# Gate matrices of the expert layer from bfloat16 one-hots, eight tokens at a time, made on VectorE

## The chip, the core and the metric

The kernel runs on one NeuronCore of one Trainium2 chip. The time is device microseconds of one execution from start to end; the median of the runs counts. A core has five engines with queues of their own: TensorE (PE; its weight loads are listed apart as PEld), VectorE (DVE), ScalarE (ACT), GpSimd (POOL) and SyncE (SP), which here only issues DMAs.

## What is computed

Two transformer blocks over 512 tokens of width 1024, in float32. The change lies in the expert layer of the first block. There each token gets, from each of 8 heads, 16 experts out of 128 x 128, each with a softmax weight; expert number 128 i + j is found from two lists of 128 sub-keys.

```
fv, fi = lax.top_k(cand, PEER_TOPK)
idx = jnp.take_along_axis(cidx, fi, axis=-1)
g = jax.nn.softmax(fv, axis=-1)
a = jax.nn.gelu(jnp.einsum('chkd,cd->chk', u_tab[idx], xc), approximate=False)
out = jnp.einsum('chkd,chk->cd', v_tab[idx], g * a)
```

A token thus has 128 triples (i, j, g). Instead of gathering rows, the kernel gives each token a dense 128 x 128 gate matrix, with g at the places (i, j) that were chosen (summed, if one is chosen twice) and zero elsewhere.

## The kernel before, in words

The first block's mixers come first, then the expert layer, then the second block. Float32 products that need full accuracy are split: `wload` (L125) loads a weight (SP), rounds it to `whi` on ScalarE (L130) and takes the rest `wlo` on VectorE (L132), and `mm3` (L135) makes three matmuls (L136 to L138) of the parts.

In the expert layer token tile 0 (128 tokens) gathers the rows of its experts: `gather_steps` (L458) has 256 steps, each an indirect DMA from POOL (L464, L473) and a sum over 1024 elements on VectorE (L466, L475). The other three tiles meet all experts densely. `h_block` (L445) computes the activations of 128 experts for 384 tokens: one `wload`, 24 matmuls of 384 columns, and one Gelu on ScalarE (L450). 68 such blocks are made during the routing and are parked in HBM (L455, `park_blocks`).

`decode` (L540) turns a tile's top-16 lists into three 128 x 128 arrays with a token's selections along the row: i, j and the weight g. It transposes them on TensorE (L584), and ScalarE copies the result out as `sT` (L586) and, negated, as `nT` (L588). After that a partition is a selection and a column is a token.

`gate_matrix` (L591) makes the gates of 16 tokens; it is called 8 times for each of tiles 1 to 3, 24 times in all. It works in chunks of 8 tokens. VectorE compares the row `io` of 0 to 127 with the 8 tokens' j: `oj`, 8 x 128 float32 (L596). For each token `og` is made, the one-hot of i times g: on VectorE in one operation (L606) or on ScalarE in two (L609, L610); `ON_DVE` (L30) says which of four tokens go to VectorE: two in tile 1, three in tiles 2 and 3. One matmul with `oj` as weights and `og` as the moving operand (L612) gives the token's 128 x 128 matrix. Four of them fill a PSUM bank, ScalarE copies the bank into `stg`, where the tokens are innermost (L614), and after 16 tokens SP stores 1 MB into `wdr` in HBM (L615).

What orders the work: the calls stand in program order, and a scheduler at build time orders each engine's instructions, with what comes first in the program preferred. After each `gate_matrix` come one or two parked blocks (`PARKS`, L26) and up to three gather steps (`GATH`, L27), and the decodes of tiles 0, 2 and 3 stand between groups (`DECODE`, L29). After the last group the parked blocks that are left follow, then the dense phase from L705, whose order is written out by hand: it reads `wdr` back, 8 rows of experts at a time, multiplies the activations by it and makes the product with the second expert table. It needs PSUM banks that the gate matrices use until their end.

Of the kernel before, what the change touches and what calls it, by code (L numbers as in the profile page):

```python
# [22 lines left out]
NEG = -1e30  # L23
NPARK = 68                                # blocks of expert activations computed during the routing
NLEAD = 3                                 # blocks in front of the parked ones
PARKS = ((), (2, 1), (2, 2), (2, 1))      # parked blocks per group of a tile's gate matrix, even and odd  # L26
GATH = (0, 1, 3, 3)                       # gathers per group of a tile's gate matrix  # L27
RATE = (0.9, 2.5)                         # gathers per dense block, parked and not
DECODE = {(1, 1): 0, (1, 4): 2, (2, 3): 3}  # L29
ON_DVE = ((), (0, 2), (0, 1, 2), (0, 1, 2))  # L30
INV_FREQ = [1.0, 0.1939227432012558, 0.03760603070259094, 0.007292664609849453,
# [10 lines left out]
def body(ctx: ExitStack, tc: tile.TileContext, A: dict, out: bass.AP):  # L42
# [13 lines left out]
    def sqrt_ahead(after):  # L56
        """Has the activation table of Sqrt loaded before the chain that needs it."""
        w = sm.tile([128, 1], F32, name="warm", bufs=1)
        SC.activation(w, after, AF.Square)
        SC.activation(w, w, AF.Sqrt)  # L60
# [13 lines left out]
    def rstd_newton(var, which):  # L74
        """1 / sqrt(var + eps) by three Newton steps from the exponent-halving guess, on the vector engine alone."""
        w = sm.tile([128, 4], F32, name="nw")
        x, y, a, r = [w[:, k:k + 1] for k in range(4)]
        V.tensor_scalar(x, var, (1e-5, 1e-6)[which], None, op0=OP.add)
        V.tensor_scalar(a.bitcast(U32), x.bitcast(U32), 1, None, op0=OP.logical_shift_right)
        V.tensor_scalar(y.bitcast(U32), a.bitcast(U32), -1.0, 1597463007.0, op0=OP.mult, op1=OP.add)  # L80
        for c in (-3.0, -12.0, -768.0):
            V.scalar_tensor_tensor(a, x, y, y, op0=OP.mult, op1=OP.mult)
            V.scalar_tensor_tensor(y, a, c, y, op0=OP.add, op1=OP.mult)
        V.tensor_scalar(r, y, -1.0 / 8192.0, None, op0=OP.mult)
        return r
# [14 lines left out]
    def first_half(junk_pool, y):  # L100
        """mean square of a row's first half, halved, plus the norm's eps"""
        ss = sumsq(junk_pool, y, 512)
        b = sm.tile([128, 1], F32, name="half")
        V.tensor_scalar(b, ss, 1.0 / D, 1e-6, op0=OP.mult, op1=OP.add)
        return b
# [49 lines left out]
    def halves(mm_pool, srcs, xh, xl, fill, parts=(0, 1)):  # L155
        """The blocks of srcs, two token tiles ahead of the other two; fill() readies those."""
        ws = [wload(src, [128, ND, 128]) for src in srcs]
        pss = [mm_pool.tile([128, S], F32, name="mm", tag="mm") for _ in srcs]
        for part in parts:
            sl = slice(part * 256, part * 256 + 256)  # L160
            if part == parts[1]:
                fill()
            for (wh, wl), ps in zip(ws, pss):
                fm_block(ps[:, sl], wh, wl, xh[:, :, sl], xl[:, :, sl], ND)
        return pss
# [25 lines left out]

    # ------------------------------------------------ first block: mixers
    with ExitStack() as st:
# [201 lines left out]

    # ------------------------------------------------ product-key experts
    # token tile 0 gathers its expert rows; the other tiles meet every expert on the tensor engine
    with ExitStack() as st:
# [87 lines left out]
        with mix as s1:  # L486
# [18 lines left out]
            for hp_ in range(16):  # L505
# [19 lines left out]
                if hp_ % 2 == 0:  # L525
                    continue
                # a pair (a, b) has (a + 1)(b + 1) - 1 pairs before it in the order, so b < 4 once a >= 4
                h = hp_ // 2
# [11 lines left out]
            def decode(t):  # L540
# [42 lines left out]
                for k, y in enumerate((sel[0], sel[1], gw)):  # L583
                    PE.transpose(tp[:, k, :], y, ident)  # L584
                sT = rt.tile([128, 3, 128], F32, name="sT", bufs=2)
                SC.activation(sT, tp[:, 0:3, :], AF.Copy)  # L586
                nT = rt.tile([128, 3, 128], F32, name="nT", bufs=2)
                SC.activation(nT, tp[:, 0:3, :], AF.Copy, scale=-1.0)  # L588
                return sT, nT

            def gate_matrix(t, q, sT, nT):  # L591
                stg = rw.tile([128, 128, TG], F32, name="stg", bufs=2)
                for c in range(TG // 8):
                    t8 = q * TG + 8 * c
                    oj = rw.tile([128, 8, 128], F32, name="oj", bufs=2)
                    V.tensor_tensor(oj, io[:, None, :].to_broadcast([128, 8, 128]),  # L596
                                    sT[:, 1, t8:t8 + 8, None].to_broadcast([128, 8, 128]), op=OP.is_equal)
                    for e in range(2):
                        pool, tag = ((psw, "wps"), (pmm, "mm"))[e]
                        ps = pool.tile([128, 4, 128], F32, name="wps", tag=tag)  # L600
                        for k in range(4):
                            tok = t8 + 4 * e + k
                            dve = k in ON_DVE[t]
                            og = rw.tile([128, 128], F32, name="og", tag="ogv" if dve else "oga", bufs=6)
                            if dve:
                                V.tensor_scalar(og, io, sT[:, 0, tok:tok + 1], sT[:, 2, tok:tok + 1],  # L606
                                                op0=OP.is_equal, op1=OP.mult)
                            else:
                                SC.activation(og, io, AF.Abs, bias=nT[:, 0, tok:tok + 1])  # L609
                                SC.activation(og, og, AF.Relu, scale=nT[:, 2, tok:tok + 1],  # L610
                                              bias=sT[:, 2, tok:tok + 1])
                            PE.matmul(ps[:, k, :], lhsT=oj[:, 4 * e + k, :], rhs=og)  # L612
                        o = 8 * c + 4 * e
                        SC.activation(stg[:, :, o:o + 4].rearrange("p i t -> p t i"), ps, AF.Copy)  # L614
# [5 lines left out]
            quick.close()  # L620
            rw = s1.enter_context(tc.tile_pool(name="rw", bufs=2, reuse_waits="tile"))
            ahead = {1: decode(1)}
            for t in range(1, NT):
                for q in range(128 // TG):
                    if (t, q) in DECODE:
                        n = DECODE[t, q]
                        ahead[n] = decode(n)
                    gate_matrix(t, q, *ahead[t])
            spread(parks, NPARK)

# [116 lines left out]

    # ------------------------------------------------ second block
    with ExitStack() as st:
# [347 lines left out]
```

## Time and profile before

| | |
|---|---|
| median of 3 runs | 2314.72 us (2312.84 to 2319.04) |
| span of the profiled execution | 2313.5 us (its page has no other time) |
| TensorE, matmuls | 2246.8 us busy, 97% of the span |
| VectorE | 1495.2 us, 65% |
| ScalarE | 986.1 us, 43% |
| GpSimd | 382.4 us, 17% |
| gate matrices (first to last matmul of L612) | 589.9 to 874.9 us |

The span runs from the first to the last instruction. A busy time is the time in which an engine had an instruction in work; matmuls overlap, so the duration of one is longer than the step from one start to the next, and in a run the step is what counts. "Idle before" names the time an engine stood still ahead of a group and what it waited for. The clock is TensorE's granted clock as a share of full speed.

### The profile page before, as it was taken

What the parts mean: (1) busy time and instruction counts of PE and PEld (TensorE: products, weight loads), DVE (VectorE), ACT (ScalarE), POOL (GpSimd) and SP (SyncE); (2) the same over time, 40 slices, a digit from 0 to 9 for tenths busy, and PEclk for the clock granted to TensorE, in tenths of its full rate; (3) what the DMA queues carried; (4) which work ended last, traced back from release to release, by engine and by line L of the source; (5) the groups of instructions that cost most, each with busy time, mean ns of one, the idle gap of its engine ahead of it and who ended that gap; (6) DMA issues with size and microseconds to landing.
All of it is one profiled execution on the core that took longest, in us unless ns stands there. A gap on an engine that the chain in (4) does not pass through costs nothing.

```text
span 2313.5 us, 30184 instructions
## 1 busy us (share of the span) xinstructions
PE 2246.8 (97%) x11337; PEld 1931.4 (83%) x11337; DVE 1495.2 (65%) x2998; ACT 986.1 (43%) x1631; POOL 382.4 (17%) x261
## 2 busy tenths in 40 slices
PE   7999998999899999999999999999999999999998
PEld 6768887989799999777779999999976778888886
DVE  4553254989999994767777777777784555333323
ACT  4354233333897783333333333333353364322222
POOL 0000000000222430323323444444400000000000
PEclk9999999999899999999999999999999999999999
DMA  5202232443577997889899898889732112333331
GB/s 173 92 19 75 90 111 84 128 125 118 213 272 289 363 350 253 295 311 329 293 323 322 306 320 297 296 302 323 274 113 74 56 55 87 105 101 93 98 100 65
DMA packets 177572, 444.82 MB, mean 192 GB/s; under 512 B 15249, under 2 KB 84241, under 8 KB 174353
## 3 DMA queue, kind: packets, MB, share of 16 engines
q1 hardware_dynamic: 140560, 308.65, 39.8%
q0 software_dynamic: 36864, 134.23, 16.3%
q8 instruction: 89, 1.46, 0.2%
q14 instruction: 59, 0.48, 0.1%
HBM read 402.19 MB, written 40.63 MB: 191 GB/s over the span
## 4 chain that ended last, share of the span: by engine, by line
PE 86%; DVE 5%; ACT 4%; DMA 4%; issue 1%; DVEq 0%; ACTq 0%; SPq 0%
PE mm L136 13%; PE mm L137 12%; PE mm L138 12%; PE hps L138 7%; PE hps L136 7%; PE hps L137 7%; PE acc L136 6%; PE acc L138 6%; PE acc L137 6%; DMA wraw<-in_v_experts_dram 3%; PE wps L612 2%; PE sc L311 1%; PE pv L346 1%; ACT stg L614 1%; PE sc L889 1%
## 5 line engine op out<-in xcount | busy, mean ns | idle before, releaser
L130 ACT ACTIVATE whi<-wraw 128x1024 fp32r<-128x1024 f32 x232 | 241.8, 1045 | 568.9 <-PE mm L137 343.0
L132 DVE TENSOR_TENSOR wlo<-wraw,whi 128x1024 fp32r<-128x1024 f32 x232 | 278.7, 1204 | 265.9 <-ACT whi L130 261.5
L136 PE MATMUL hps<-x2h,whi 128*128 128x384 f32 x1024 | 348.1, 340 | 2.1 <-ACT whi L130 1.8
L138 PE MATMUL hps<-x2h,wlo 128*128 128x384 f32 x1024 | 345.1, 337 | 0.8 <-DVE wlo L132 0.8
L137 PE MATMUL hps<-x2l,whi 128*128 128x384 f32 x1024 | 344.2, 336 | 0.0
L464 POOL DMA_INDIRECT gu<-in_u_experts_dram,ix x128 | 190.8, 1491 | 914.0 <-PE wps L612 605.5
L136 PE MATMUL acc<-whi,hh 128*128 128x512 f32 x768 | 302.6, 394 | 17.3 <-ACT hh L117 17.3
L138 PE MATMUL acc<-whi,hl 128*128 128x512 f32 x768 | 303.2, 395 | 0.0
L137 PE MATMUL acc<-wlo,hh 128*128 128x512 f32 x768 | 302.7, 394 | 0.0
L664 DVE TENSOR_TENSOR wlo<-wraw,whi 128x1024 fp32r<-128x1024 f32 x188 | 227.5, 1223 | 74.6 <-ACT whi L662 69.0
L662 ACT ACTIVATE whi<-wraw 128x1024 fp32r<-128x1024 f32 x188 | 198.3, 1056 | 171.3 <-issue 85.5
L473 POOL DMA_INDIRECT gv<-in_v_experts_dram,ix x128 | 189.7, 1482 | 380.7 <-DVE hres L475 275.3
L136 PEld LDWEIGHTS hps<-x2h,whi 128*128 128x128 f32 x1024 | 193.3, 189 | 5.4 <-ACT whi L130 2.1
L137 PEld LDWEIGHTS hps<-x2l,whi 128*128 128x128 f32 x1024 | 193.1, 189 | 2.7
L138 PEld LDWEIGHTS hps<-x2h,wlo 128*128 128x128 f32 x1024 | 193.1, 189 | 1.1 <-DVE wlo L132 1.1
L136 PEld LDWEIGHTS acc<-whi,hh 128*128 128x128 f32 x768 | 145.5, 189 | 49.6 <-ACT hh L117 21.0
L138 PEld LDWEIGHTS acc<-whi,hl 128*128 128x128 f32 x768 | 145.8, 190 | 33.3 <-DVE hl L118 2.7
L137 PEld LDWEIGHTS acc<-wlo,hh 128*128 128x128 f32 x768 | 145.7, 190 | 29.3
L475 DVE SCALAR_TENSOR_TENSOR hres<-gv,ga,hres 128x1024 f32<-128x1024 f32 x128 | 164.1, 1282 | 1.0
L466 DVE CUSTOM_DVE_ANT_0 gu<-gu,xtok 128x1024 f32<-128x1024 f32 x128 | 154.5, 1222 | 0.0
L137 PE MATMUL mm<-x4l,whi 128*128 128x512 f32 (+1 forms) x384 | 143.9, 375 | 0.0
L136 PE MATMUL mm<-x4h,whi 128*128 128x512 f32 (+1 forms) x384 | 143.3, 376 | 0.3 <-ACT x4h L117 0.3
(316 smaller groups left out, 4022.3 us busy)
## 6 DMA issues: line engine op xcount, KB each, us to landing
wraw<-in_u_cols_dram SPq DMA_DIRECT2D x128, 512.0 KB
wraw<-in_v_experts_dram SPq DMA_DIRECT2D x128, 512.0 KB
wraw<-in_w_in_dram SPq DMA_DIRECT2D x50, 512.0 KB
wdr<-stg SPq DMA_DIRECT2D x24, 1024.0 KB
wt<-wdr SPq DMA_DIRECT2D x16, 1536.0 KB
park<-hg SPq DMA_DIRECT2D x68, 192.0 KB
hg<-park SPq DMA_DIRECT2D x68, 192.0 KB
wraw<-in_w_gate_dram SPq DMA_DIRECT2D x22, 512.0 KB
```

Of the source, the lines that this page charges most:

```text
L130: SC.activation(hi, raw, AF.Copy)
L132: V.tensor_tensor(lo, raw, f(hi), op=OP.subtract)
L136: PE.matmul(ps, lhsT=ah, rhs=bh, start=start, stop=False)
L137: PE.matmul(ps, lhsT=ah, rhs=bl, start=False, stop=False)
L138: PE.matmul(ps, lhsT=al, rhs=bh, start=False, stop=stop)
L464: GP.indirect_dma_start(out=u, out_offset=None, in_=A["u_experts"], in_offset=bass.IndirectOffsetOnAxis(ap=ix[:, s_:s_ + 1], axis=0))
L466: V.tensor_tensor_reduce(out=u, in0=u, in1=xtok, scale=1.0, scalar=0.0, op0=OP.mult, op1=OP.add, accum_out=a[:, s_:s_ + 1])
L473: GP.indirect_dma_start(out=v, out_offset=None, in_=A["v_experts"], in_offset=bass.IndirectOffsetOnAxis(ap=ix[:, s_:s_ + 1], axis=0))
L475: V.scalar_tensor_tensor(hres[:, 0, :], v, a[:, s_:s_ + 1], hres[:, 0, :], op0=OP.mult, op1=OP.add)
L612: PE.matmul(ps[:, k, :], lhsT=oj[:, 4 * e + k, :], rhs=og)
L662: SC.activation(hi, raw, AF.Copy)
L664: V.tensor_tensor(lo, raw, f(hi), op=OP.subtract)
```

## The change

`decode` copies i, j and g as bfloat16 (`sT`, five rows of 128): i and j are whole numbers below 128, g is kept as the sum of three bfloat16, each the rest that the one before it leaves. ScalarE makes the first copy, VectorE the two rests in four operations. `nT` is gone. `gate_matrix` makes, for a chunk of 8 tokens, the one-hots of i and of j in one VectorE operation (`hot`) and the three products of the first with the parts of g in another (`og`), in a layout with the 8 tokens innermost. Each token then takes three bfloat16 matmuls that add up in PSUM, whose operands step over the 8 tokens. `io8`, the numbers 0 to 127 each eight times, is made once. The ScalarE path and `ON_DVE` are gone. Apart from this only comments change.

```diff
@@ -582,34 +581,34 @@
                 tp = psw.tile([128, 4, 128], F32, name="wps", tag="wps")
                 for k, y in enumerate((sel[0], sel[1], gw)):
                     PE.transpose(tp[:, k, :], y, ident)
-                sT = rt.tile([128, 3, 128], F32, name="sT", bufs=2)
-                SC.activation(sT, tp[:, 0:3, :], AF.Copy)
-                nT = rt.tile([128, 3, 128], F32, name="nT", bufs=2)
-                SC.activation(nT, tp[:, 0:3, :], AF.Copy, scale=-1.0)
-                return sT, nT
-
-            def gate_matrix(t, q, sT, nT):
+
+                sT = rt.tile([128, 5, 128], BF16, name="sT", bufs=2)
+                SC.activation(sT[:, 0:3, :], tp[:, 0:3, :], AF.Copy)
+                rest = rt.tile([128, 128], F32, name="grest")
+                V.tensor_tensor(rest, tp[:, 2, :], sT[:, 2, :], op=OP.subtract)
+                V.tensor_copy(sT[:, 3, :], rest)
+                V.tensor_tensor(rest, rest, sT[:, 3, :], op=OP.subtract)
+                V.tensor_copy(sT[:, 4, :], rest)
+                return sT
+
+            def gate_matrix(t, q, sT):
                 stg = rw.tile([128, 128, TG], F32, name="stg", bufs=2)
                 for c in range(TG // 8):
                     t8 = q * TG + 8 * c
-                    oj = rw.tile([128, 8, 128], F32, name="oj", bufs=2)
-                    V.tensor_tensor(oj, io[:, None, :].to_broadcast([128, 8, 128]),
-                                    sT[:, 1, t8:t8 + 8, None].to_broadcast([128, 8, 128]), op=OP.is_equal)
+                    ts = slice(t8, t8 + 8)
+                    hot = rw.tile([128, 2, 128, 8], BF16, name="hot")
+                    V.tensor_tensor(hot, io8[:, None, :, :].to_broadcast([128, 2, 128, 8]),
+                                    sT[:, 0:2, None, ts].to_broadcast([128, 2, 128, 8]), op=OP.is_equal)
+                    og = rw.tile([128, 3, 128, 8], BF16, name="og")
+                    V.tensor_tensor(og, hot[:, 0, None, :, :].to_broadcast([128, 3, 128, 8]),
+                                    sT[:, 2:5, None, ts].to_broadcast([128, 3, 128, 8]), op=OP.mult)
                     for e in range(2):
                         pool, tag = ((psw, "wps"), (pmm, "mm"))[e]
                         ps = pool.tile([128, 4, 128], F32, name="wps", tag=tag)
                         for k in range(4):
-                            tok = t8 + 4 * e + k
-                            dve = k in ON_DVE[t]
-                            og = rw.tile([128, 128], F32, name="og", tag="ogv" if dve else "oga", bufs=6)
-                            if dve:
-                                V.tensor_scalar(og, io, sT[:, 0, tok:tok + 1], sT[:, 2, tok:tok + 1],
-                                                op0=OP.is_equal, op1=OP.mult)
-                            else:
-                                SC.activation(og, io, AF.Abs, bias=nT[:, 0, tok:tok + 1])
-                                SC.activation(og, og, AF.Relu, scale=nT[:, 2, tok:tok + 1],
-                                              bias=sT[:, 2, tok:tok + 1])
-                            PE.matmul(ps[:, k, :], lhsT=oj[:, 4 * e + k, :], rhs=og)
+                            for p in range(3):
+                                PE.matmul(ps[:, k, :], lhsT=hot[:, 1, :, 4 * e + k], rhs=og[:, p, :, 4 * e + k],
+                                          start=(p == 0), stop=(p == 2))
                         o = 8 * c + 4 * e
                         SC.activation(stg[:, :, o:o + 4].rearrange("p i t -> p t i"), ps, AF.Copy)
                 SY.dma_start(wdr[(t - 1) * (128 // TG) + q], stg)
@@ -619,13 +618,15 @@
 
             quick.close()
             rw = s1.enter_context(tc.tile_pool(name="rw", bufs=2, reuse_waits="tile"))
+            io8 = rw.tile([128, 128, 8], BF16, name="io8", bufs=1)
+            V.tensor_copy(io8, io[:, :, None].to_broadcast([128, 128, 8]))
             ahead = {1: decode(1)}
             for t in range(1, NT):
                 for q in range(128 // TG):
                     if (t, q) in DECODE:
                         n = DECODE[t, q]
                         ahead[n] = decode(n)
-                    gate_matrix(t, q, *ahead[t])
+                    gate_matrix(t, q, ahead[t])
             spread(parks, NPARK)
 
         dn = st.enter_context(tc.tile_pool(name="dn", bufs=2, reuse_waits="tile"))
```

## Rows read from the trace of the kernel before

**Rows 1.** The page, part 1: busy time, share of the span and instructions of each engine.

```profile
span 2313.5 us, 30184 instructions
...
PE 2246.8 (97%) x11337; PEld 1931.4 (83%) x11337; DVE 1495.2 (65%) x2998; ACT 986.1 (43%) x1631; POOL 382.4 (17%) x261
```

**Rows 2.** Windows of the gate stage: length, busy (instructions) per engine, clock, DMA share, GB/s.

```profile
587.00:691.00 104.00, 94.05 (x581) 90.08 (x582) 95.90 (x178) 97.92 (x200) 26.08 (x17) 0.94 0.71 253
691.00:794.00 103.00, 102.15 (x673) 100.91 (x672) 101.61 (x185) 79.07 (x144) 31.96 (x23) 1.00 0.88 323
794.00:877.00 83.00, 82.84 (x563) 82.15 (x562) 77.59 (x150) 64.80 (x114) 26.78 (x19) 1.00 0.94 348
877.00:900.00 23.00, 23.00 (x135) 23.00 (x134) 7.36 (x6) 8.25 (x11) 0.00 (x0) 1.00 0.83 272
```

**Rows 3.** Groups by shape, window 586:877: count, busy us, mean ns, idle before and its releasers.

```profile
L614 ACT ACTIVATE stg<-wps 128x512 f32<-128x512 f32 x96 | 101.9, 1079 | 2.5 <-PE wps L612 2.5
L612 PE MATMUL wps<-og,oj 128*128 128x128 f32 x768 | 99.5, 284 | 9.0 <-ACT og L610 6.9 <-DVE og L606 2.0
L612 PEld LDWEIGHTS wps<-og,oj 128*128 128x128 f32 x768 | 94.4, 196 | 14.5 <-ACT og L610 9.8 <-DVE og L606 2.1 <-PE hps L137 1.1
L606 DVE TENSOR_SCALAR og<-io,sT 128x128 f32<-128x128 f32 x256 | 72.0, 354 | 5.2 <-PE wps L612 3.9 <-PE hps L138 1.3
...
L596 DVE TENSOR_TENSOR oj<-io,sT 128x1024 f32<-128x1024 f32 x48 | 58.6, 1221 | 2.9 <-PE wps L612 2.8
L610 ACT ACTIVATE og<-og,sT,nT 128x128 f32<-128x128 f32 x128 | 58.2, 488 | 0.5
...
L609 ACT ACTIVATE og<-io,nT 128x128 f32<-128x128 f32 x128 | 46.2, 395 | 0.0
```

**Rows 4.** Time line of SyncE's queue in tile 3: start, duration, issue.

```profile
805.51 0.32 SPq L615 DMA_DIRECT2D wdr<-stg  x1
...
817.61 0.32 SPq L615 DMA_DIRECT2D wdr<-stg  x1
...
825.66 0.32 SPq L615 DMA_DIRECT2D wdr<-stg  x1
```

**Rows 5.** Time line of TensorE, tile 2: a block's matmuls, then the gate products.

```profile
749.72 0.33 PE L136 MATMUL hps<-x2h,whi 128*128 128x384 f32 x1
...
751.28 3.73 PE L612 MATMUL wps<-og,oj 128*128 128x128 f32 x32
754.77 0.42 PE L136 MATMUL hps<-x2h,whi 128*128 128x384 f32 x1
```

**Rows 6.** Time lines of TensorE: products of 512 columns; further on, products of 64.

```profile
1019.70 0.39 PE L138 MATMUL acc<-whi,hl 128*128 128x512 f32 x1
...
1023.78 0.39 PE L138 MATMUL acc<-whi,hl 128*128 128x512 f32 x1
...
1791.78 2.00 PE L915 MATMUL pv<-va,pt 128*128 128x64 f32 x16
```

**Rows 7.** Groups by shape, whole span: ScalarE's dense copy of 512 elements.

```profile
L520 ACT ACTIVATE rsc<-sc 128x512 f32<-128x512 f32 x16 | 9.6, 597 | 17.5 <-PE sc L518 17.5
```

**Rows 8.** Time line of VectorE in tile 2: one chunk and the next one's start.

```profile
752.21 1.63 DVE L606 TENSOR_SCALAR og<-io,sT 128x128 f32<-128x128 f32 x6
753.75 1.22 DVE L596 TENSOR_TENSOR oj<-io,sT 128x1024 f32<-128x1024 f32 x1
754.88 1.63 DVE L606 TENSOR_SCALAR og<-io,sT 128x128 f32<-128x128 f32 x6
```

**Rows 9.** Groups by shape, window 586:877: VectorE's bfloat16 operations in the decode.

```profile
L560 DVE TENSOR_TENSOR eq<-abf,io 128x2048 bf16<-128x2048 f32 x6 | 13.6, 2284 | 0.0
L563 DVE TENSOR_TENSOR eq<-eq,sif 128x2048 bf16<-128x2048 bf16 x6 | 7.2, 1218 | 0.0
L565 DVE TENSOR_TENSOR eq<-eq 128x1024 bf16<-128x1024 bf16 x6 | 4.0, 686 | 0.0
```

**Rows 10.** The same view: a small operation of the decode on 128 columns.

```profile
L576 DVE TENSOR_TENSOR gw<-gw,gs 128x128 f32<-128x128 f32 x3 | 0.9, 289 | 0.0
```

More of the change, by code (lines that the diff above doesn't have):

```diff
@@ L29 @@
 DECODE = {(1, 1): 0, (1, 4): 2, (2, 3): 3}
-ON_DVE = ((), (0, 2), (0, 1, 2), (0, 1, 2))
 INV_FREQ = [1.0, 0.1939227432012558, 0.03760603070259094, 0.007292664609849453,
```

## The prediction

> **What bounds the kernel now.** I read the page's first part, then the stretches of the stage that the change touches, then the groups of instructions in that stage, then time lines of TensorE and VectorE inside it. The page says that TensorE has work in 97% of the span [rows 1], so time comes mostly from TensorE's list of work, and an edit elsewhere counts only where TensorE waits. The gate matrices are made from about 587 to 877 us, in 24 groups of 16 tokens, eight groups for each of three token tiles. By tile the stage takes 104, 103 and 83 us [rows 2]. What to see there: in the first tile ScalarE is busy 97.92 of 104 us, TensorE 94.05, and its mean granted clock is 0.94. In the other two tiles TensorE is busy 102.15 of 103 and 82.84 of 83, ScalarE has a quarter free. VectorE is busy 95.90, 101.61 and 77.59, so it is nearly full everywhere: 275.1 of 290. So the first tile waits for ScalarE's half of the one-hots (the weight loads of L612 stood idle 14.5 us, most of it behind the og of L610 [rows 3]); the other two are TensorE's, with VectorE a hair behind. The start times of the gate stores in tile 3 show it: a group with two parked blocks takes 12.1 us, one with a single block 8.1 [rows 4]. The difference, 4.0, is one block of 24 matmuls at 0.173 us [rows 5]; the rest is the group's own matmuls.
>
> **Part 1, the matmuls.** The 384 products show as 768 float32 instructions of 128 columns [rows 3], two to a product. A run of 32 takes 3.49 us until the next block starts, 0.109 each; with its last result taken off, (3.73 - 0.28) / 31 = 0.111 [rows 5]. So 768 x 0.111 = 85 us of TensorE. The new code issues 3 x 384 = 1152 instructions, each with a weight load of its own, as today even two successive products of one weight have. What one bfloat16 instruction costs no row shows, so bounds. Below: split float32 products of 384 columns start every 0.173 us (1.56 over nine) and of 512 every 0.227 (4.08 over eighteen) [rows 5, 6]; so 128 columns in one pass are 0.054, and 0.173 - 3 x 0.054 = 0.011 stays per instruction: 0.065, which makes 75 us, 10 less than now. The float32 row is 0.111, two passes, and it does not fall with fewer columns: sixteen of 64 columns take 2.00 us, 0.115 each [rows 6], so there the weights set the pace.
>
> What speaks for the upper half is the layout. Both operands now step over eight tokens, 16 bytes from one element to the next, where today's are dense. The one strided writer in the stage pays for it: ScalarE's copy of 512 elements into the gate tile, in steps of 64 bytes, takes 1079 ns [rows 3], a dense copy of the same size from the same memory 597 [rows 7], 1.8 times as much. TensorE reading at twice the time per element would be at the pace of the float32 row, 0.111 to 0.12. Upper bound: the float32 row times 1.8, 0.20, or 231 us. I take 0.112, because the strided row is the only one that shows what such steps cost and a read of two passes is a row of this engine: 1152 x 0.112 = 129 us, **44 more than now**. [...]
>
> **Part 2, VectorE.** Removed in each chunk of eight tokens: one oj, started 1.13 us before what follows, and six og in 1.54 us in tiles 2 and 3 (752.21, 753.75, 754.88) [rows 8], together 2.67; in tile 1 only four og, about 2.16. Added: hot, 2048 bfloat16 elements, and og, 3072. The nearest rows are the decode's bfloat16 products: 2048 elements 1218 ns, 1024 elements 686, one of the two sources repeated in the first; with a float32 source 2284 [rows 9]. By their slope og is 1218 + 532 = 1750. Less 0.08 for the overlap that oj shows (1221 ns long [rows 3], next start after 1.13), a chunk is 1.14 + 1.67 = 2.81. That is 0.65 more in 16 chunks and 0.14 more in 32: 15 us. The decode's four new small operations on 128 columns, at about 0.29 each [rows 10], are 1.2 us in each of three tiles, and io8 about one oj, 1.1 us, once. Sum: **19 us more**, 294 us for a stage of 290. The other end, with no gain from bfloat16, is 2284 + 3426 ns per chunk: 131 us more than the 2.81.
>
> **Part 3, ScalarE.** Gone are 46.2 + 58.2 us of og [rows 3] and the negated copy. Of its 242 us some 137 stay. This pays only where TensorE waited for it: 290 - 279.0 = 11 us idle in the stage, and about 6 us of lost speed in tile 1 (granted 0.94 of 104 us) [rows 2]. What is late next is VectorE's og: it needs hot, and the four or eight products of a chunk need it, and behind a waiting product on TensorE stand parked blocks. hot and og have two buffers each, so VectorE's third hot waits for TensorE, and behind it stand the next wlo and the gathers' sums, whose buffers GpSimd waits for. Two chunks are one group, about 12 us ahead, which covers the two blocks of 4.1 us between groups. No DMA is added on SP's or POOL's queue, and stores and loads keep their order.
>
> **Sum.** TensorE's stage at full clock is 279.0 - 6.2 = 273 us; with 44 it is 317. At the start the new decode and io8 lie on the way to the first product, about 2 us, and I leave 1 us of other waits. 320 us against 290 is +30, and VectorE's 294 fits under it with room. Behind 877 the order is fixed and TensorE bounds, so all of it reaches the end: 2313.5 + 30 = 2344 of the profiled span. The page gives a span and no other time for that execution; the median of the runs, 2314.72, lies 1.2 above. **2345 us.**
>
> **Rivals.**
> - *VectorE becomes the bound.* If strided reads cost nothing, TensorE's stage is 273 - 10 = 263 and VectorE's 294 plus some 3 of waits lasts longer: 297 against 290, +7, about 2322, between +3 and +14. For it: VectorE is at 95% today and its new sum is sure in kind. It holds up to a matmul of about 0.09 us. Half of this case is within the 0.3%, 7 us, that a measurement here can tell from no change. Chance 0.28.
> - *Faster, the gathers step aside.* With 0.065 per product TensorE has 263 us of work, and no wait for ScalarE. It gains if VectorE sheds at least 26 of its 294 us: gathers that lag into 877 to 900, where VectorE is busy 7.36 of 23 [rows 2]. Then 263 + 2 + 3 = 268, -22, about 2293. Against it: the gathers stand ahead of the next group in program order, only 16 us are free there, and products must cost the lower bound. Chance 0.11.
> - *Far slower.* The bfloat16 operations don't run at the rate of the rows, so the change doesn't do what it says: 294 + 131 = 425, about 2451. Or products at the upper bound: 273 + 146 = 419, about 2445. Against the first: the decode's row with a repeated operand is at the faster rate [rows 9]. Chance 0.09 for both.
>
> **The numbers.** The forecast, TensorE bound by strided operands, has 0.52; its own range, for a matmul of 0.105 to 0.125, is 121 to 144 us, +22 to +45, or 2337 to 2360. The range of all reaches from most of VectorE's case up to it, 2315 to 2361, and leaves out about 0.2: the faster and the far slower. Faster 0.11; same 0.13, nearly all from VectorE's case; slower 0.52 + 0.15 + 0.09 = 0.76.
>
> **What will show it.** In the profile after: L612's successor with 1152 instructions, starts in a run 0.112 apart (0.065 for the first two rivals); TensorE at 99% of the stage and VectorE near 92%; hot near 1.22 and og near 1.75 us (2.3 and 3.4 for the far slower case); ScalarE's og gone and no wait for it in tile 1; groups of tile 3 at about 13.7 and 9.6 us in place of 12.1 and 8.1; the last gate store near 905 us. I am wrong if products run dense-fast and VectorE is at 100% with gaps on TensorE, or if the stage ends before 877.

## The result and the profile after

The kernel after takes 2535.89 us (median of 4 runs, 2533.67 to 2538.88), the kernel before 2315.99 on the same chip (4 runs, 2312.84 to 2319.04). The ratio is 1.0951 with a 95% interval of 1.0934 to 1.0968: 220 us slower. The forecast was 2345 with a range of 2315 to 2361, so the sign was right and the size was not, by a factor of seven.

The page after, part 1 and the clock row of part 2. To compare with [rows 1]: TensorE keeps its 97% of a span that is 222 us longer, VectorE falls from 65% to 60%, ScalarE from 43% to 36%. The clock row (tenths of full speed in 40 equal slices) falls from 9 to 7 just where the gate matrices are made.

```profile
span 2535.2 us, 30445 instructions
...
PE 2470.9 (97%) x11721; PEld 2056.0 (81%) x11721; DVE 1513.4 (60%) x2803; ACT 919.0 (36%) x1372; POOL 374.5 (15%) x261
...
PEclk9999999997777777799999999999999999999999
```

The clock row of the kernel before:

```profile
PEclk9999999999899999999999999999999999999999
```

The window of the whole gate stage after (length, busy time and instructions of PE, PEld, DVE, ACT, POOL, clock, DMA share, GB/s), to set against [rows 2]. The stage is 508 us and not 290. VectorE, busy 275 of 290 before, now stands still for 217 of 508. TensorE is busy in nearly all of it, at a mean granted clock of 0.74.

```profile
587.00:1095.00 508.00, 500.24 (x2202) 393.69 (x2201) 290.91 (x316) 175.71 (x198) 77.96 (x59) 0.74 0.50 171
```

Groups by shape in the window 586:1110, the answer to [rows 3]. `hot` and `og` last what was forecast, 1223 and 1751 ns, and VectorE waits 161.8 us for TensorE's products (L610). Nothing of weight stands idle before the products any more: 6.1 us, all for `og`. ScalarE's copies wait 192.1 us for them.

```profile
L610 PE MATMUL wps<-og,hot 128*128 128x128 bf16 x1152 | 277.0, 414 | 6.1 <-DVE og L603 6.1
L610 PEld LDWEIGHTS <-hot 128*128 128x128 bf16 x1152 | 164.9, 146 | 107.3 <-DVE og L603 6.3 <-issue 6.0 <-DVE wlo L131 0.7
...
L613 ACT ACTIVATE stg<-wps 128x512 f32<-128x512 f32 x96 | 103.5, 1080 | 196.4 <-PE wps L610 192.1 <-issue 3.9 <-ACT hg L449 0.4
...
L603 DVE TENSOR_TENSOR og<-hot,sT 128x3072 bf16<-128x3072 bf16 x48 | 82.9, 1751 | 0.0
L600 DVE TENSOR_TENSOR hot<-io,sT 128x2048 bf16<-128x2048 bf16 x48 | 58.7, 1223 | 161.8 <-PE wps L610 161.8
```

TensorE's time line (start, duration) in the eighth group, the last of tile 1, which answers to [rows 5]. A run of 48 products takes 11.05 us until the block behind it starts. With the last one's result taken off, (11.42 - 0.41) / 47 = **0.234 us** for each, where 0.112 was taken. The block that follows starts its matmuls of 384 columns every 0.32 us, and every 0.17 some three microseconds later. The granted clock was 0.50 from 751.6 to 752.9 us and 1.00 from 755 to 758.

```profile
740.39 0.34 PE L137 MATMUL hps<-x2h,wlo 128*128 128x384 f32 x1
740.57 11.42 PE L610 MATMUL wps<-og,hot 128*128 128x128 bf16 x48
751.62 0.68 PE L135 MATMUL hps<-x2h,whi 128*128 128x384 f32 x1
...
752.43 0.52 PE L137 MATMUL hps<-x2h,wlo 128*128 128x384 f32 x1
752.75 0.52 PE L135 MATMUL hps<-x2h,whi 128*128 128x384 f32 x1
...
754.90 0.33 PE L136 MATMUL hps<-x2l,whi 128*128 128x384 f32 x1
755.07 0.34 PE L137 MATMUL hps<-x2h,wlo 128*128 128x384 f32 x1
```

SyncE's stores of tile 3, which answer to [rows 4]: groups of 20.7 and 17.3 us in place of 12.1 and 8.1.

```profile
995.96 0.32 SPq L614 DMA_DIRECT2D wdr<-stg  x1
1016.67 0.32 SPq L614 DMA_DIRECT2D wdr<-stg  x1
1033.93 0.32 SPq L614 DMA_DIRECT2D wdr<-stg  x1
```

**Where the 222 us are.** I added the steps from each TensorE start to the next, from the first product to the last (589.9 to 875.0 before, 597.8 to 1093.4 after). The products rise from 92.1 to 269.6 us: +177.5. The parked blocks' matmuls between them rise from 192.4 us (1020 of them) to 225.5 (991): +33. Of these 225.5 us, 102.8 lie at half clock (granted 0.50); at 0.173 instead of 0.32 a matmul they would have been 56, so the clock costs about 47 us (an estimate), and 14 come back through fewer matmuls and fewer waits. The first product starts 8 us later. That makes 218.5; the last 3 us arise behind the stage.

The 8 us at the start are on two engines. VectorE now does two `wlo` before the steps that finish `gw`, so that `gw` is ready at 588.06 us (L575) in place of 585.83 (L576). Its transposition on TensorE, at 585.89 before, then stands behind a parked block's matmuls, which run at half clock (granted 0.50 from 586.0 to 590.3), until 590.32. Then the four new decode operations on VectorE (L588 to L591) take turns with two `hot` and the next decode's work, so that 4.7 us lie between the first of them and the first `og`.

```profile
590.00 0.52 PE L137 MATMUL hps<-x2h,wlo 128*128 128x384 f32 x1
590.32 0.41 PE L583 MATMUL wps<-ident,gw 128*128 128x128 f32 x1
```

```profile
591.29 0.29 DVE L588 TENSOR_TENSOR grest<-wps,sT 128x128 f32<-128x128 f32 x1 [0.76 <-ACT sT L586]
...
595.98 3.42 DVE L603 TENSOR_TENSOR og<-hot,sT 128x3072 bf16<-128x3072 bf16 x2
```

### The profile page after: what moved, and what is told of

Read it like the earlier page. It is cut to its first block, busy times and chain, and to the rows that moved or that the text cites. A ratio compares the mean times of both kernels' runs of the same rounds, so it can differ in the third digit from the quotient of the medians.

```text
span 2535.2 us, 30445 instructions
## 1 busy us (share of the span) xinstructions
PE 2470.9 (97%) x11721; PEld 2056.0 (81%) x11721; DVE 1513.4 (60%) x2803; ACT 919.0 (36%) x1372; POOL 374.5 (15%) x261
## 3 DMA queue, kind: packets, MB, share of 16 engines
q8 instruction: 92, 1.51, 0.2%
## 4 chain that ended last, share of the span: by engine, by line
PE 90%; DMA 4%; DVE 3%; ACT 1%; issue 1%; SPq 0%; DVEq 0%; ACTq 0%
PE mm L135 11%; PE mm L136 11%; PE mm L137 11%; PE wps L610 11%; PE hps L135 7%; PE hps L137 7%; PE hps L136 7%; PE acc L135 6%; PE acc L137 6%; PE acc L136 6%; DMA wraw<-in_v_experts_dram 4%; PE sc L310 1%; PE pv L345 1%; PE sc L890 1%; PE pv L916 1%
## 5 line engine op out<-in xcount | busy, mean ns | idle before, releaser
L135 PE MATMUL hps<-x2h,whi 128*128 128x384 f32 x1024 | 369.6, 361 | 1.9 <-ACT hg L449 1.8
L137 PE MATMUL hps<-x2h,wlo 128*128 128x384 f32 x1024 | 365.4, 358 | 1.2 <-DVE wlo L131 1.2
L136 PE MATMUL hps<-x2l,whi 128*128 128x384 f32 x1024 | 362.5, 354 | 0.0
L610 PE MATMUL wps<-og,hot 128*128 128x128 bf16 x1152 | 277.0, 414 | 6.1 <-DVE og L603 6.1
L610 PEld LDWEIGHTS <-hot 128*128 128x128 bf16 x1152 | 164.9, 146 | 107.3 <-DVE og L603 6.3
L135 PEld LDWEIGHTS hps<-x2h,whi 128*128 128x128 f32 x1024 | 209.5, 205 | 8.5 <-ACT hg L449 4.2
L137 PEld LDWEIGHTS hps<-x2h,wlo 128*128 128x128 f32 x1024 | 207.9, 203 | 3.1 <-DVE wlo L131 1.5
L136 PEld LDWEIGHTS hps<-x2l,whi 128*128 128x128 f32 x1024 | 208.1, 203 | 2.8
L613 ACT ACTIVATE stg<-wps 128x512 f32<-128x512 f32 x96 | 103.5, 1080 | 196.4 <-PE wps L610 192.1
```

What stands on the lines that cost most here:

```text
L135: PE.matmul(ps, lhsT=ah, rhs=bh, start=start, stop=False)
L136: PE.matmul(ps, lhsT=ah, rhs=bl, start=False, stop=False)
L137: PE.matmul(ps, lhsT=al, rhs=bh, start=False, stop=stop)
L610: PE.matmul(ps[:, k, :], lhsT=hot[:, 1, :, 4 * e + k], rhs=og[:, p, :, 4 * e + k], start=(p == 0), stop=(p == 2))
```

## The experiments

Each diff is against the kernel after unless it says otherwise. "One run" means a single time beside the kernel before on the same chip, 2317.95 us for the first four and a median of 2314.32 (13 runs) for the next four.

**e1, e2, e3: how far apart the elements lie.** The layout keeps TI tokens innermost in place of 8, so a matmul steps over 8, 4 or 2 bytes (dense) in place of 16. The decode writes its lists in the same order, with three copies on ScalarE in place of one; the same products are made, from as many matmuls.

```diff
+TI = 4      # e2: 2, e3: 1
...
+NB = 8 // TI
...
-hot = rw.tile([128, 2, 128, 8], BF16, name="hot")
+hot = rw.tile([128, NB, 2, 128, TI], BF16, name="hot")
...
-og = rw.tile([128, 3, 128, 8], BF16, name="og")
+og = rw.tile([128, NB, 3, 128, TI], BF16, name="og")
...
+n, b = divmod(4 * e + k, TI)
...
-PE.matmul(ps[:, k, :], lhsT=hot[:, 1, :, 4 * e + k], rhs=og[:, p, :, 4 * e + k],
+PE.matmul(ps[:, k, :], lhsT=hot[:, n, 1, :, b], rhs=og[:, n, p, :, b],
```

> [...] Operations and their counts are the same (48 hot, 48 og, 1152 bfloat16 matmuls). The changed kernel's products start 0.234 us apart. [...] Theory B (the cost grows with the step): about half of the excess goes, 0.12 to 0.16 us apart, total 2390 to 2450 us. Theory C (the step has no part in it; three matmuls that add up in one PSUM area wait for each other, or bfloat16 products are slow): 0.234 us as before, total about 2535 us.

> [...] Theory B: 0.08 to 0.11 us. Theory C: 0.234 us, 2535 us.

> As the run with two tokens innermost, but with the tokens outermost: both operands of the products are dense. [...] Theory C: 0.234 us. VectorE repeats its second source along the innermost dimension here; I expect it to lose the faster rate: hot 2.3 and og 3.4 us, so that VectorE bounds the stage at about 425 us, total about 2450 us; if it keeps the rate, total about 2325 us.

Measured in one run each: 2364.84, 2338.55 and 2444.26 us. TensorE's time lines of e1 (8 bytes), e2 (4 bytes) and e3 (dense), each a run of products and, for the first two, the block behind it:

```profile
716.16 5.83 PE L622 MATMUL wps<-og,hot 128*128 128x128 bf16 x48
721.75 0.43 PE L136 MATMUL hps<-x2h,whi 128*128 128x384 f32 x1
```

```profile
701.51 2.94 PE L622 MATMUL wps<-og,hot 128*128 128x128 bf16 x48
704.25 0.42 PE L136 MATMUL hps<-x2h,whi 128*128 128x384 f32 x1
```

```profile
718.26 1.51 PE L622 MATMUL wps<-og,hot 128*128 128x128 bf16 x24
```

The steps are 5.59 / 48 = 0.116, 2.74 / 48 = 0.057, and (1.51 - 0.22) / 23 = 0.056; the median over all products is 0.118, 0.057 and 0.056. So four bytes cost nothing, eight double the time, sixteen double it again. That is neither "any step costs the same" nor "the step has no part in it" (theory C): the cost is graded with the step, as theory B has it. Theory B's sizes were too high, though: at 4 bytes it gave 0.08 to 0.11 us, and at 8 bytes a total of 2390 to 2450. At 16 bytes, in the kernel after, the pace is the same at both: median 0.234 us for 620 steps at a granted clock of 0.50 and for 462 at 1.00. So there something other than TensorE's granted clock sets the pace. Dense it differs. In e3 a run ahead of a block whose matmuls start 0.32 us apart takes 2.50 us for 24 products, 0.104 each:

```profile
705.68 2.74 PE L622 MATMUL wps<-og,hot 128*128 128x128 bf16 x24 [0.99 <-DVE og L613]
708.18 0.67 PE L138 MATMUL hps<-x2h,wlo 128*128 128x384 f32 x1
708.64 0.52 PE L136 MATMUL hps<-x2h,whi 128*128 128x384 f32 x1
708.97 0.52 PE L137 MATMUL hps<-x2l,whi 128*128 128x384 f32 x1
```

e2 also shows what is left of the change without the price of the steps: it is still 21 us slower than the kernel before. Its window of the gate stage, and waits in it (who waited for what, us in total, times, longest):

```profile
597.00:897.00 300.00, 260.73 (x2158) 249.45 (x2158) 275.62 (x297) 161.02 (x195) 113.35 (x57) 0.94 0.79 279
```

```profile
ACT whi L130 <- DMA wraw<-in_u_cols_dram: 69.6, 25, 6.2
...
PE hps L136 <- ACT hg L450: 24.9, 12, 4.0
...
PE wps L622 <- DVE og L613: 14.1, 7, 8.1
```

VectorE is busy 276 of 300 us and TensorE stands idle for 39. Part of it waits for `og`; the larger part is the parked blocks, which are late as well: ScalarE, which rounds their weights to `whi`, waits 69.6 us for them to arrive. In e3 the products are at their best and the kernel is slower than e2 by 106 us, because `hot` and `og`, with the repeated source innermost, lose their fast rate: 2285 and 3350 ns, where e2 has 1219 and 1751. Groups by shape of e3, whole span, and its window of the stage:

```profile
L613 DVE TENSOR_TENSOR og<-hot,sg 128x3072 bf16<-128x3072 bf16 x48 | 159.6, 3350 | 0.0
L608 DVE TENSOR_TENSOR hot<-io,sij 128x2048 bf16<-128x2048 bf16 x48 | 108.7, 2285 | 0.4 <-issue 0.4
```

```profile
597.00:1001.00 404.00, 295.75 (x2169) 275.80 (x2169) 403.57 (x299) 168.28 (x196) 177.22 (x58) 0.85 0.61 208
```

VectorE has next to no gap in 404 us. The layout of 8 tokens buys VectorE's rate and pays on TensorE; a layout of two has both (0.057 us a product, 1219 and 1751 ns).

**e4, e5: which operand it is.** One-hots of i and of j in tiles of their own, so that the two can differ. In e4 the weights step over 4 bytes and the moving operand over 16; in e5 it is the other way round.

```diff
+TI = 8      # e5: 2
+TW = 2      # e5: 8
...
-hot = rw.tile([128, 2, 128, 8], BF16, name="hot")
+hot = rw.tile([128, NB, 128, TI], BF16, name="hot")
...
+hoj = rw.tile([128, 8 // TW, 128, TW], BF16, name="hoj")
...
-PE.matmul(ps[:, k, :], lhsT=hot[:, 1, :, 4 * e + k], rhs=og[:, p, :, 4 * e + k],
+PE.matmul(ps[:, k, :], lhsT=hoj[:, nw, :, bw], rhs=og[:, n, p, :, b],
```

> Only the weights (one-hot of j) are laid out with a step of 4 bytes, the moving operand keeps its step of 16 bytes; VectorE makes the two one-hots in two operations of 1024 elements, some 0.15 us more per chunk. If the moving operand alone pays: 0.234 us per product still, total about 2535 us. If the weights alone pay: 0.065 to 0.08 us, total about 2330 us. If each pays half, one after the other: about 0.12 to 0.15 us, total 2400 to 2440 us. Theory C: 0.234 us.

> The mirror of the run with the weights alone in pairs: here the moving operand steps 4 bytes, the weights keep their 16. That run left products 0.229 us apart, so the moving operand by itself sets the changed kernel's pace. If weights at 16 bytes cost nothing: products 0.057 us apart as with pairs on both sides, total about 2345 us (VectorE has one operation more per chunk). If the weight load is slowed as the moving read is but hidden under it before: near 0.2 us apart, total 2500 us. In between (the load of weights took 146 ns in the changed kernel, 103 in the run with pairs): 0.12 to 0.15 us, total 2390 to 2430 us.

Measured in one run each: 2524.0 and 2344.57 us. TensorE's time line and the weight loads' group of e4, then of e5:

```profile
713.98 11.15 PE L628 MATMUL wps<-og,hoj 128*128 128x128 bf16 x48
724.76 0.68 PE L137 MATMUL hps<-x2h,whi 128*128 128x384 f32 x1
```

```profile
L628 PEld LDWEIGHTS <-hoj 128*128 128x128 bf16 x1152 | 138.5, 123 | 122.0 <-issue 4.1 <-DVE hoj L614 2.1 <-DVE og L618 1.7
```

```profile
705.99 3.27 PE L628 MATMUL wps<-og,hoj 128*128 128x128 bf16 x48
709.07 0.42 PE L137 MATMUL hps<-x2h,whi 128*128 128x384 f32 x1
```

```profile
L628 PEld LDWEIGHTS <-hoj 128*128 128x128 bf16 x1152 | 82.0, 148 | 21.3 <-DVE og L618 16.1 <-issue 3.0 <-DVE wlo L133 0.6
```

The weight loads' group of e2, to compare:

```profile
L622 PEld LDWEIGHTS <-hot 128*128 128x128 bf16 x1152 | 73.2, 103 | 21.6 <-DVE og L613 16.5 <-issue 4.0 <-DVE ga L466 0.3
```

With the moving operand at 16 bytes the median step is 0.229, nearly that of the kernel after; with only the weights at 16 bytes it is 0.064, nearly that of e2. A weight load at 16 bytes takes 148 ns, 45 more than e2's 103, and almost all of it lies beside the products. It is the moving operand. For 8 bytes the two operands were not parted.

**e6: one product in place of three.** The kernel after's layout, and only the first of the three matmuls, so the gates keep one bfloat16 part. It takes away two thirds of the products and nothing of VectorE's work.

```diff
-for p in range(3):
+for p in range(1):
     PE.matmul(...)
```

> The changed layout with its steps of 16 bytes and all of VectorE's work, but only the first of the three matmuls of a token is issued, so the gate keeps its first bfloat16 part alone. 384 products at 0.234 us are 90 us, what the kernel before spends on its products. If the slower clock after these products (granted 0.74 over the changed kernel's stage) comes from how few columns they stream per time, it stays low here while they run and the parked blocks after them pay again: mean granted clock in the stage under 0.85, total 2345 to 2375 us. If the clock falls only because of the long runs of 24 to 48 products: clock near 0.95, total as with pairs, about 2338 us, bound by VectorE.

Measured in one run: 2351.05 us. The 384 products start 0.234 us apart as before (the median; with the waits among them they take 96.3 us), so their price hangs neither on their number nor on adding up in PSUM. 768 products fewer took 185 us from the time; 768 x 0.234 is 180. Windows of e6, the stage and 104 us at its start:

```profile
597.00:913.00 316.00, 292.81 (x1400) 250.91 (x1400) 281.11 (x300) 163.88 (x197) 114.86 (x58) 0.88 0.75 267
587.00:691.00 104.00, 88.40 (x404) 75.12 (x405) 91.78 (x117) 52.45 (x65) 14.58 (x10) 0.81 0.58 199
```

The time lies in the range of the first expectation. The clock is still down, at 0.88, though not under the 0.85 named there, and behind a run of 16 products the block's matmuls start 0.32 us apart again (at 709.55, 709.87 and 710.19). In e1, with three times as many products at 0.118, it is 0.97 over the stage. Its window:

```profile
597.00:926.00 329.00, 318.79 (x2166) 308.00 (x2166) 281.15 (x300) 171.18 (x197) 113.83 (x59) 0.97 0.74 259
```

So the lower clock goes with the slow products. It goes with gaps on TensorE too: e3, whose products are at the best pace and where TensorE, waiting for VectorE, is busy in 296 of 404 us, has 0.85. In the kernel after TensorE was busy in 500 of 508 us, so there it fell without gaps.

**e7: two float16 parts.** Pairs of tokens as in e2, and the gate as the sum of two float16, no longer exact, in 768 matmuls; `og` has 2048 elements.

```diff
+F16 = mybir.dt.float16
...
+TI = 2
...
-og = rw.tile([128, 3, 128, 8], BF16, name="og")
+og = rw.tile([128, NB, 2, 128, TI], F16, name="og")
...
-for p in range(3):
+for p in range(2):
```

> Pairs innermost and two float16 parts of the gate in place of three bfloat16 (the gate keeps some 22 bits). 768 products, og 2048 elements. In the run with pairs VectorE was busy 290 of 310 us of the stage and bound it; its chunk falls from 2.81 to 2.28 us, 25 us in 48 chunks, and TensorE's products to 44 us. If VectorE is the bound: total about 2313 us, level with the kernel before. If it was not VectorE (waits between the two engines): gain under 10 us, total 2330 us.

Measured in 3 rounds: 2316.42 us, ratio 1.0013 (1.0000 to 1.0025). A third of the products and 26 us of `og` are gone against e2, and it comes out level with the kernel before, not faster, as the first expectation has it. (VectorE's 290 of 310 us in its text are 285 in e2's trace.) Its window of the stage and TensorE's waits there:

```profile
597.00:877.00 280.00, 242.54 (x1776) 232.21 (x1774) 249.51 (x292) 157.45 (x192) 107.70 (x58) 0.91 0.82 299
```

```profile
PE hps L137 <- ACT hg L451: 23.6, 9, 5.5
PE wps L621 <- DVE og L612: 9.4, 4, 7.0
```

TensorE has 37 us to spare in 280 and waits for blocks and for `og`; VectorE is the fuller.

**e8, e9, e10: fewer gathers among the groups.** Sixteen of tile 0's gather steps, each a DMA and a sum on VectorE, move from the gate stage into the dense phase, with two float16 parts (e8), in the kernel before with nothing else (e9), and with pairs and the three exact parts (e10).

```diff
-GATH = (0, 1, 3, 3)
-RATE = (0.9, 2.5)
+GATH = (0, 1, 2, 2)
+RATE = (0.9, 2.8)
```

> As the run with two float16 parts, and 16 gather steps fewer are placed in the stage (two per group in place of three in tiles 2 and 3), which the dense phase takes (2.8 in place of 2.5 per block that is not parked). 20 us of VectorE's work leave the stage. If VectorE bounds the stage and has room in the dense phase: 10 to 18 us below the run with two parts, about 2298 us. If the dense phase is bound by its gathers: no gain or a loss there, 2313 us or more.

> The kernel before with nothing changed but the placing of the gathers, as in the run that was 29 us faster: two per group in tiles 2 and 3, 2.8 per block that is not parked. It tells how much of those 29 us the placing brings alone. If TensorE bounds tiles 2 and 3, as the rows of before say (busy 102.15 of 103 and 82.84 of 83), and ScalarE tile 1: within 5 us of the kernel before, 2310 to 2318 us. If VectorE was the bound: 15 us or more below it, 2300 us or less.

> The run with pairs innermost and three bfloat16 parts, with the gathers placed as in the run before. With pairs VectorE was 285 us busy in a stage of 310; 20 us of it leave. If VectorE bounds: 2338 - 20 = 2318 us or a little above the kernel before; if the two engines' waits for each other go with it, as they did in the run with float16 (31 us for 20 us of work): 2307 us.

Measured in 3 rounds each: e8 2285.22 us, ratio 0.9875 (0.9855 to 0.9895); e9 2325.86, 1.0046 (1.0029 to 1.0063); e10 2305.44, 0.9956 (0.9939 to 0.9973). In the kernel before the move does harm: 10.6 us, which neither of e9's expectations allows, with TensorE idle for 8 us between 691 and 794 us behind `og` (L606). Why `og` is later there I didn't settle. With pairs the same move brings 31 us (e8 against e7, where 10 to 18 were expected) and about 30 (e10 against e2, each beside the kernel before on its own chip), near the second of e10's expectations. So neither the pairs nor the move is a gain alone, and together they are one. e10 is exact and faster than both kernels, than the kernel before by 0.4%. Its window, and the waits that answer to e2's:

```profile
597.00:865.00 268.00, 247.57 (x2153) 240.11 (x2153) 261.24 (x274) 162.28 (x196) 102.07 (x43) 0.98 0.81 288
```

```profile
ACT whi L130 <- DMA wraw<-in_u_cols_dram: 23.2, 15, 3.1
...
PE wps L622 <- DVE og L613: 15.8, 8, 8.1
...
PE hps L136 <- ACT hg L450: 3.7, 3, 2.0
```

VectorE is still the fullest engine, busy 261 of 268 us where e2 has 276 of 300. What TensorE no longer waits for is not `og` (14.1 us in e2, 15.8 here) but the parked blocks (24.9 and 3.7), and their weights arrive sooner. A gather that moves takes its sum off VectorE and its transfer off the DMA engines; no run parts the two, so which of them had kept the blocks late is not shown.

**e11, e12: fewer still.** e8 and e10 with another step of the same kind.

```diff
-GATH = (0, 1, 2, 2)
-RATE = (0.9, 2.8)
+GATH = (0, 0, 1, 2)
+RATE = (0.95, 2.95)
```

> Two float16 parts with still fewer gathers in the stage: none in tile 1, one per group in tile 2, two in tile 3 (24 in place of 39), 0.95 and 2.95 per dense block. In the run with 39 TensorE already set the groups of tile 3 (10.3 and 6.0 us), so only tiles 1 and 2 can gain: VectorE 19 us less there, of which about 8 us reach the end, 2277 us. If the dense phase can't take more gathers: 2285 us or above.

> Pairs and three bfloat16 parts as in e10, with still fewer gathers between the groups, (0, 0, 1, 2) per group and (0.95, 2.95) per dense block, as e11 has them. In e10 VectorE was busy 261 of the 268 us of the stage and TensorE 248, and the kernel took 2305.4. If VectorE's load in the stage is what holds it, eleven or more of its sums of 1.2 us leave it, and the stage ends 8 to 14 us sooner: 2291 to 2298. The rival: TensorE's own 248 us and the waits between chunks hold it already, and the sums that move into the dense phase cost there what they save here: within 3 us of e10, 2302 to 2309.

Measured in 3 rounds each: e11 2281.77 us, 0.9856 (0.9839 to 0.9872); e12 2301.66, 0.9936 (0.9920 to 0.9953). The windows of e11's and of e12's stage:

```profile
597.00:834.00 237.00, 224.24 (x1768) 218.04 (x1767) 218.40 (x249) 158.52 (x195) 48.53 (x28) 0.97 0.82 297
```

```profile
597.00:848.00 251.00, 238.55 (x2086) 232.73 (x2086) 242.98 (x251) 156.18 (x190) 54.27 (x28) 0.99 0.79 278
```

e12's last product starts at 852.0 us and e10's at 863.2: 11 us, within the 8 to 14 of the theory that VectorE held it. The time falls by only 4, to the edge of the rival's range, and the intervals of e10 and e12 overlap. In the profiles 3 us of the 11 are given back in the dense phase (the last expert product starts 7.8 us sooner) and 3 behind it. In e11, whose time lies between its two expectations, TensorE has the larger load, 224 of 237; in e12 TensorE and VectorE are busy 239 and 243 of 251. So the second step is worth little: VectorE no longer holds the stage alone, and the moved steps seem to cost something where they go. e11 has the lowest median of all, with gates of two float16 parts, and e12 the lowest of the exact ones; their intervals overlap those of e8 and e10.

## Why the prediction was wrong

**The step that failed is Part 1, the price of a product: 0.112 us was taken and 0.234 measured**, 270 us and not 129. The direction was argued from the right place, the strided operands. The size was taken over from another engine: ScalarE's factor of 1.8 for a strided copy [rows 3, 7], read as "twice the time per element", and then set equal to the float32 row. e1 and the kernel after show that for TensorE there is no single factor: 8 bytes cost 2.1 times the dense 0.056, 16 bytes 4.2 times. Even the "upper bound", 0.20, failed; it multiplied a float32 row by ScalarE's factor, so it was no bound but a second estimate from the same wrong ratio. The lower bound, 0.065, was no bound either: where nothing is paid for steps, e3 and e2 show 0.056 and 0.057, so most of the 0.011 that the sum kept for each instruction is not there.

**A term was missing: the clock.** The sum kept TensorE at full clock and even took 6 us back for tile 1. The products' own rows fell to half clock, which cost them nothing (0.234 us at a granted 0.50 as at 1.00), but the parked blocks between them then ran at 0.32 us a matmul, in place of 0.173, for a while: about 47 us, an estimate from the steps above. The prediction did not ask what slow products do to the work beside them.

e1 checks the rest of the sum, since its products are nearly at the price I took. TensorE's stage there is 325 us against the forecast 317; 1152 x 0.006 = 7 of the 8 is the price. The kernel is 47 us slower than before on its chip, against the forecast 30: those 8, 7 more at the start (598.8 in place of 589.9, with 2 allowed for), and 2 elsewhere.

Point by point:
- **Part 2, VectorE**: `hot` and `og` 1223 and 1751 ns, forecast 1.22 and 1.75. Right, and its sum right too: 291 us busy in the stage against 294. As forecast, VectorE did not bound.
- **Part 3, ScalarE**: the waits of L612 for ScalarE's `og` are gone, as forecast; the gain drowned. "About 2 us" at the start was wrong: 8, because `gw` is finished 2 us later, because four small operations in a full queue wait for their turn, and because TensorE's transposition stands behind blocks at half clock.
- **Groups of tile 3** at 13.7 and 9.6 us: they were 20.7 and 17.3. The difference between the two kinds, one block, was 3.4 where it had been 4.0.
- **Rival "VectorE becomes the bound"**: not the kernel after; e2, where steps cost nothing, comes nearest, at +21 and not +7. VectorE's work came out near, 276 us in the 300 of the window and 285 from 587 on, against 294. But it had gaps of 24 us where 3 were allowed for, the first product started 7 us late, and most of TensorE's idle time there was for parked blocks.
- **Rival "faster, the gathers step aside"**: they don't by themselves (e2, e7). Moved by hand they do (e10, e12), for 10 and 15 us of the 22 that were priced.
- **Rival "far slower"**: its first branch did not occur, but e3 is its test: 2285 and 3350 ns against 2284 and 3426, and 2444 us against the 2451 worked out. Its second branch, products at the upper bound, is what happened, beyond its price: at 0.09 for the two it had far too little, since the row behind it was the only one with a step in it and that one was not TensorE's.

What stays open: why the pace is graded as it is, what exactly makes the clock fall, and whether VectorE's sums or the gathers' transfers held up the parked blocks in e2. On the pace there is one estimate from e1 and the kernel after: 128 columns reach over 1024 bytes in 0.118 us at a step of 8, and over 2048 in 0.234 at 16, which is 8.7 and 8.8 bytes per ns. That a fixed rate is behind it is not shown, and no run steps further than 16 bytes.

## What to carry to other kernels

Look at the step of a matmul's moving operand before anything else in such a layout: here bfloat16 at 4 bytes was free (0.057 us a product against 0.056 dense), 8 bytes doubled and 16 quadrupled the time (0.118 and 0.234), while the weights could step 16 bytes for next to nothing (0.064). Where an elementwise engine wants something innermost to keep its fast rate, two tokens may be enough: `hot` took 1.22 us with two, four and eight, and 2.29 with the repeat innermost. More only moves the bill to TensorE. When one engine is eased, see what the others wait for next and try moving optional work in the same edit: here neither the pairs nor the moved gathers gained anything alone.

## What the runs showed of the hardware

A product of 128 bfloat16 columns with a weight load of its own starts every 0.056 us dense, 0.057 with both operands at 4 bytes, 0.118 with both at 8 and 0.234 with both at 16. At 16 bytes it is 0.234 at a granted clock of 0.50 and at 1.00; dense it was 0.104 over 24 products ahead of a block whose matmuls of 384 columns started 0.32 us apart, where others start 0.173 apart. With the moving operand alone at 16 bytes it is 0.229. Weights alone at 16 bytes load in 148 ns in place of 103 and raise the step to 0.064. In a stage of 508 us, 270 of them products at 16 bytes and most of the rest matmuls of 384 columns, TensorE was busy in 500 and had a mean granted clock of 0.74; with the products at 8 bytes it was 0.97. VectorE's two-byte operation on a source repeated along the dimension next to innermost kept its rate with an inner run of 8, 4 and 2 elements (1.22 us for 2048, 1.75 for 3072) and lost it when the repeat was innermost (2.29 and 3.35).
